# A two-layer hybrid decoder trunk: the order in which branch steps and projections are emitted, the lanes of the gated heads, and the width of the inverse steps

## The chip, the core and the metric

The kernel runs on one core of a Trainium2 chip. The metric is device time in microseconds (us) of one execution. Five engines work side by side, each in the order of its own instruction stream: TensorE (PE, with its weight loads shown as PEld), VectorE (DVE), ScalarE (ACT), GpSimd (POOL), and SyncE (SP), which issues nearly all DMAs.

## The reference

Sequence 512, width 1024, two layers, all in float32:

```python
for layer in range(DEPTH):
    u = rms_norm(h, norm_mix_g[layer])
    p_a, p_b, p_c, p_gate = _split(u @ w_in[layer], ...)
    y_a = rwkv7_branch(p_a, ...)    # 8 heads of 64, a linear recurrence over time
    y_b = hgrn2_branch(p_b, ...)    # 4 gated heads, keys and values of 128
    y_c = dsa_branch(p_c, cos, sin) # 8 heads of 64, top 128 keys chosen by an indexer
    branch = jnp.einsum('bsnc,ncd->bsnd', jnp.stack([y_a, y_b, y_c], axis=2), w_branch[layer])
    merged = jnp.sum(sigmoid(p_gate) * branch, axis=2)
    h = h + merged @ w_o[layer]
    h = h + conv_glu(rms_norm(h, norm_ffn_g[layer]), ...)  # up, 3-tap convolution, silu gate, down
return rms_norm(h, norm_final_g)
```

## The kernel before

All activations lie as 128 features by 512 time steps. A large product is made of three matmuls for each block of 128 input features (`big`, L293): a value is split into a high part and a residual (`split`, L264: ACT copies the high part, DVE or POOL subtracts), and high by high, high by residual and residual by high are summed in a bank of PSUM named `acc`. Such a matmul has 128x512 results; this text calls it a **wide matmul**. A projection of 128 columns is a block of 24 of them. Weights come in by SP as `wraw`; ACT makes `whi` and POOL `wlo` from them (`wload`, L270), five buffers of each, two pairs to a block.

A layer has a mixer and a feed-forward part. In the mixer two kinds of work are emitted into one stream by `interleave` (L62). **Fills** are made of wide matmuls: the projections of pair i of branch a (`pa0` to `pa3`), of branch c (`pc`) and of gated head i (`pb0` to `pb3`), the gates `gb` and `ga`, and the merges `mc`, `mb`, `ma`. **Lanes** are chains of small matmuls, each of which needs what DVE or ACT made of the one before: `pair_a` (L663, steps a0 to a3), `select` (s1 to s3), `attend` (c0 to c3) and `head_b` (L1004, b0 to b3). Lane steps write PSUM tiles named `lane`, all other wide work `acc`. Each `yield` of a lane gives a hand-written number, the us after which its next step may be emitted; PE's clock for that is a `Meter` that adds up a price for each matmul. While no lane is due, one fill goes on.

What emits first does not fix the order fully: the framework's scheduler then orders each engine's stream by priority, with work under `prio("feed")` ahead of the rest, and allots tile buffers (tag `t` has `NT` = 39 of them, 512 floats by 128 partitions each). At run time each engine takes its own stream strictly in order.

Names that the prediction uses:

- `pair_a`: `ars` (statistics by eleven DVE instructions of `rsqrt`, L248), `rx`, then `AR` and `BK` (L726 to L733), the masked 32x32 system `NU`/`TX`, its inverse by four doublings (L851 to L866: 32 small PE matmuls, a DVE multiply, 32 more, a DVE add and a 32x32-block transpose), a loop over eight chunks of 64 time steps (tiles `p1d`, `uf`, `VV`, `BKn`, `sbd`), and a normalization that ends in `yn` (L942), which PE transposes.
- `head_b`: nine levels of `bX` and `bE` (L1024 to L1086), four PE products of the upper levels, then `brs` and `bon` (L1115), again transposed by PE.
- Both layers begin with five projections made of the input before its norm is known (`feed["left"]`, L1240); meanwhile DVE makes the normed input `us`, then `uh` and `ul` from it. The feed-forward part does the same over four blocks (L1316), its `ul` on POOL from tiles `fu`.

## Time and profile before

| | us |
|---|---|
| median of three runs | 2244.77 |
| lowest and highest | 2241.41, 2249.47 |
| the profiled execution, its own time | 2235.76 |
| its span, first to last instruction | 2233.9 |
| PE busy in the span | 2113.2 |
| DVE, ACT, POOL busy | 1218.0, 1051.4, 944.3 |

The profiled execution is one run; its durations are set against its own 2235.76 us. A matmul's busy time reaches to the modelled end of its result, and the next one begins before that, so PE can be called busy and still lose time between starts. Two of the wide matmuls start 0.227 us apart when nothing is in their way.

### The profile page before, as it was taken

What the parts mean: (1) busy time and instruction counts of PE and PEld (TensorE: products, weight loads), DVE (VectorE), ACT (ScalarE), POOL (GpSimd) and SP (SyncE); (2) the same over time, 40 slices, a digit from 0 to 9 for tenths busy, and PEclk for the clock granted to TensorE, in tenths of its full rate; (3) what the DMA queues carried; (4) which work ended last, traced back from release to release, by engine and by line L of the source; (5) the groups of instructions that cost most, each with busy time, mean ns of one, the idle gap of its engine ahead of it and who ended that gap; (6) DMA issues with size and microseconds to landing.
All of it is one profiled execution on the core that took longest, in us unless ns stands there. A gap on an engine that the chain in (4) does not pass through costs nothing.

```text
span 2233.9 us, 41570 instructions
## 1 busy us (share of the span) xinstructions
PE 2113.2 (95%) x16598; PEld 1670.0 (75%) x16598; DVE 1218.0 (55%) x2744; ACT 1051.4 (47%) x2016; POOL 944.3 (42%) x739
## 2 busy tenths in 40 slices
PE   8998999998899999999999899999888999999997
PEld 6676777776687788888877677777666877888886
DVE  8668894467725633331185788753875356333211
ACT  6455555455433444443345564555563344444321
POOL 4231232232364666554442312222224547656563
PEclk9998999999999999999999999999999999999998
DMA  6221222222246233334332212222222552333332
GB/s 196 54 74 31 83 62 80 77 62 68 66 149 174 69 105 102 96 90 121 107 100 54 65 40 76 59 83 76 67 62 85 153 154 85 95 95 99 92 97 71
DMA packets 323506, 199.71 MB, mean 89 GB/s; under 512 B 10096, under 2 KB 304240, under 8 KB 323312
## 3 DMA queue, kind: packets, MB, share of 16 engines
q1 hardware_dynamic: 322592, 196.00, 30.3%
q8 instruction: 131, 2.15, 0.4%
q10 hardware_dynamic: 720, 1.05, 0.1%
q14 instruction: 63, 0.52, 0.1%
HBM read 178.14 MB, written 18.87 MB: 88 GB/s over the span
## 4 chain that ended last, share of the span: by engine, by line
PE 73%; DVE 17%; ACT 5%; issue 3%; POOL 2%; DMA 0%; SPq 0%; DVEq 0%; ACTq 0%; POOLq 0%
PE acc L55 59%; PE lane L55 12%; PE lane L59 1%; DVE bX L1048 1%; DVE sc L574 1%; DVE m L573 1%; DVE bX L1054 1%; DVE h L453 1%; ACT whi L265 1%; DVE bE L1052 1%; POOL ul L266 1%; DVE bF L1056 1%; POOL wlo L266 1%; DVE ars L254 0%; DVE rt L451 0%
## 5 line engine op out<-in xcount | busy, mean ns | idle before, releaser
L266 POOL TENSOR_TENSOR wlo<-wraw,whi 128x512 fp32r<-128x512 f32 (+1 forms) x602 | 789.6, 1313 | 1238.9 <-ACT whi L265 1129.9
L55 PE MATMUL acc<-uh,whi 128*128 128x512 f32 (+1 forms) x1776 | 727.7, 410 | 3.0 <-ACT uh L1263 2.9
L55 PE MATMUL acc<-ul,whi 128*128 128x512 f32 (+1 forms) x1776 | 712.3, 401 | 13.8 <-POOL ul L266 6.7
L55 PE MATMUL acc<-uh,wlo 128*128 128x512 f32 (+1 forms) x1776 | 708.1, 399 | 0.6 <-POOL wlo L266 0.6
L265 ACT CAST whi<-wraw 128x512 fp32r<-128x512 f32 (+1 forms) x604 | 368.9, 612 | 660.7 <-PE acc L55 558.9
L55 PEld LDWEIGHTS acc<-ul,whi 128*128 128x128 f32 (+1 forms) x1776 | 337.7, 190 | 80.7 <-POOL ul L266 8.9
L55 PEld LDWEIGHTS acc<-uh,whi 128*128 128x128 f32 (+1 forms) x1776 | 338.1, 190 | 79.2 <-issue 10.0
L55 PEld LDWEIGHTS acc<-uh,wlo 128*128 128x128 f32 (+1 forms) x1776 | 337.6, 190 | 69.9 <-POOL wlo L266 1.1
L1132 DVE SCALAR_TENSOR_TENSOR fc<-acc,vct,fc 128x511 f32<-128x511 f32 x80 | 60.0, 750 | 273.9 <-ACT fc L1131 273.9
L55 PE MATMUL acc<-hl,whi 128*128 128x512 f32 x416 | 162.0, 390 | 0.0
L55 PE MATMUL acc<-hh,wlo 128*128 128x512 f32 x416 | 162.0, 389 | 0.0
L55 PE MATMUL acc<-hh,whi 128*128 128x512 f32 x416 | 161.9, 389 | 0.0
L1151 DVE TENSOR_TENSOR h<-h,acc 128x512 f32<-128x512 f32 x16 | 11.0, 688 | 197.5 <-PE acc L55 197.5
L55 PEld LDWEIGHTS acc<-hl,whi 128*128 128x128 f32 x416 | 78.1, 188 | 16.3
L55 PEld LDWEIGHTS acc<-hh,wlo 128*128 128x128 f32 x416 | 78.1, 188 | 16.1
L55 PEld LDWEIGHTS acc<-hh,whi 128*128 128x128 f32 x416 | 78.1, 188 | 16.1
L55 PE MATMUL acc<-yl,whi 128*128 128x512 f32 x192 | 75.7, 394 | 3.3 <-POOL yl L266 3.2
L55 PE MATMUL acc<-yh,whi 128*128 128x512 f32 x192 | 76.2, 397 | 0.8 <-ACT yh L265 0.8
L55 PE MATMUL acc<-yh,wlo 128*128 128x512 f32 x192 | 75.3, 392 | 0.0
L55 PEld LDWEIGHTS lane<-bX 128*32 128x32 f32 (+2 forms) x1536 | 32.1, 116 | 42.2 <-issue 21.9
L55 PEld LDWEIGHTS lane<-TX,NU 32*32 32x32 f32 x4096 | 42.9, 107 | 25.8 <-issue 13.8
L1131 ACT ACTIVATE fc<-acc,vct 128x512 f32<-128x512 f32 x80 | 62.1, 776 | 0.0
(340 smaller groups left out, 3029.2 us busy)
## 6 DMA issues: line engine op xcount, KB each, us to landing
wraw<-in_w_in_dram SPq DMA_DIRECT2D x123, 512.0 KB, 3.8
wraw<-in_w_up_dram SPq DMA_DIRECT2D x88, 512.0 KB, 3.7
wraw<-in_w_down_dram SPq DMA_DIRECT2D x32, 512.0 KB, 3.9
wraw<-in_w_branch_dram SPq DMA_DIRECT2D x24, 512.0 KB, 3.4
gate<-rt SPq DMA_DIRECT2D x32, 256.0 KB, 2.0
rt<-gate SPq DMA_DIRECT2D x32, 256.0 KB, 2.9
wraw<-in_w_o_dram SPq DMA_DIRECT2D x16, 512.0 KB, 4.0
wraw<-in_w_down_dram SPq DMA_DIRECT2D x16, 384.0 KB, 3.4
```

What stands on the lines that cost most here:

```text
L55: return self.engine.matmul(out, lhsT, rhs, **kw)
L59: return self.engine.transpose(*args, **kw)
L265: act.copy(hi, src)
L266: eng.tensor_sub(lo, src, hi.bitcast(F32))
L453: dve.tensor_add(mg[d], mg[d], t_)
L573: dve.max(m8, sc[:, :S])
L574: dve.match_replace(sc[:, :S], m8, sc[:, :S], SENT)
L1048: dve.tensor_mul(Xu, qu, Eu)
L1052: dve.tensor_sub(El, end, Fl)
L1054: dve.tensor_mul(Xl, kl, El)
L1131: act.activation(c, ps, AF.Identity, bias=cw[:, 3, j:j + 1], scale=cw[:, 2, j:j + 1])
L1132: dve.scalar_tensor_tensor(c[:, 1:], ps[:, :T - 1], cw[:, 1, j:j + 1], c[:, 1:], op0=ALU.mult, op1=ALU.add)
```

## The change

`Timed` wraps DVE and ACT and adds up a price for each of their instructions (0.15 us plus 1.08 or 0.9 ns for each element of a partition). A lane's `yield` without a number now waits 0.35 us plus 1.1 times the vector work recorded since its last step; a few yields keep numbers, and the factor `PACE` of 0.9 is gone. A lane's first step comes 3.0 us after its inputs. Gates and merges yield 1.0 after each tile of 128 columns, and the next fill is then chosen anew, in the order of the list. Heads b0 and b2 now follow `select` in its lane, b1 and b3 follow `attend`; `pb0` waits for s3, `pa2` also for c2, `pb2` and `pb3` for the head two before. In `pair_a` each DVE step of the inverse takes all eight chunks in one instruction instead of four and four; `BK` is scaled in place after `Gs` on POOL, without tiles `BKs`; `bvh` and `bvl` are made later. The work beside late blocks (`side`) is issued under feed priority; a layer's start makes `us` after the first two late blocks instead of three, and the feed-forward part has six late blocks instead of four, with two tiles made beside each of the first four.

```diff
+class Timed:
+        def call(*args, **kw):
+            n = max(math.prod(a.shape[1:]) for a in (*args, *kw.values()) if isinstance(a, bass.AP))
+            self.t += self.base + self.per * n
+            return f(*args, **kw)
...
-def interleave(meter, lanes, fills):
+def interleave(meter, vectors, lanes, fills):
...
+        if wait is None:
+            wait = LATENCY + SHARE * (sum(v.t for v in vectors) - v0)
         return meter.t - t0, wait
...
-                lane[1], lane[2], lane[3] = make(), name, max(now, lane[3])
+                lane[1], lane[2], lane[3] = make(), name, max(now + START, lane[3])
...
-            lane[3] = now + (wait or 0.0) * PACE
+            lane[3] = now + max(wait, 0.0)
...
+            if wait:
                 fill = None
...
-BURST, PACE = 0.3, 0.9
+BURST, LATENCY, SHARE, START = 0.3, 0.35, 1.1, 3.0
...
+    dve, act = Timed(nc.vector, 0.15, 1.08e-3), Timed(nc.scalar, 0.15, 0.9e-3)
...
             nc.sync.dma_start(dst[d], t_)
+            yield 1.0
...
             r = use(ps)
-        if late:
-            feed["side"](feed["left"])
+            if late:
+                feed["side"](feed["left"])
...
-            for g in range(2):
-                dve.tensor_mul(X[:, 4 * g:4 * g + 4], quarter(px, g), bc(f"low{m}"))
-            yield 0.9
+            dve.tensor_mul(X, both(px), bc(f"low{m}"))
+            yield
...
-            for g in range(2):
-                cg = slice(4 * g, 4 * g + 4)
-                dve.tensor_add(Tt[:, cg], Tt[:, cg], quarter(pt, g))
-                dve.transpose(U[:, cg], Tt[:, cg])
-            yield 0.3
-            if next(parts, 0) is None:
-                yield 1.2
+            dve.tensor_add(Tt, Tt, both(pt))
+            dve.transpose(U, Tt)
+            next(parts, 0)
+            yield
...
-        yield 2.5
 
         rs = mp.tile([P, 24], F32, name=f"ars{lane}")
...
-            yield 1.5
+            yield
             if m == 16:
...
-                for k in {4: range(0, 3), 3: range(3, 6), 2: range(6, 8)}.get(left, ()):
+                for k in {4: range(0, 4), 3: range(4, 8)}.get(left, ()):
...
+            heads_b = [(f"b{i}", lambda i=i: head_b(lay, i, st, i % 2, l1, ys[1]), [f"pb{i}"]) for i in range(4)]
...
-                [(f"s{t}", lambda t=t: select(st, t, l1), ["pc"]) for t in (1, 2, 3)],
+                [(f"s{t}", lambda t=t: select(st, t, l1), ["pc"]) for t in (1, 2, 3)] + heads_b[0::2],
...
-                + [(f"b{i}", lambda i=i: head_b(lay, i, st, i % 2, l1, ys[1]), [f"pb{i}"]) for i in range(4)],
+                + heads_b[1::2],
...
-                for k in {3: range(0, 2), 2: range(2, 5), 1: range(5, 8)}.get(left, ()):
+                for k in {5: range(0, 2), 4: range(2, 4), 3: range(4, 6), 2: range(6, 8)}.get(left, ()):
...
-            feed.update(left=4, src=(gh, gl), rb=nrm.rb, tmp=lambda: fw.tile([P, T], F32, name="fc", bufs=6),
+            feed.update(left=6, src=(gh, gl), rb=nrm.rb, tmp=lambda: fw.tile([P, T], F32, name="fc", bufs=6),
```

Three places in the order show what that moves. The first is PE's stream late in a mixer, the upper levels of the last gated head, b3 of layer 0, before (`acc` rows are wide matmuls, `bX` rows the products of a level):

```order
L55 MATMUL lane_7057<-bX 64x64 x4
L55 MATMUL acc<-uh_519,whi 128x512
L55 MATMUL acc<-ul_527,whi 128x512
L55 MATMUL acc<-uh_519,wlo 128x512
L55 MATMUL lane_7077<-bX 128x128 x2
L55 MATMUL acc<-uh_520,whi 128x512
L55 MATMUL acc<-ul_528,whi 128x512
L55 MATMUL acc<-uh_520,wlo 128x512
L55 MATMUL acc<-uh_521,whi 128x512
L55 MATMUL acc<-ul_529,whi 128x512
L55 MATMUL acc<-uh_521,wlo 128x512
L55 MATMUL acc<-uh_522,whi 128x512
```

And PE's stream at the same levels of head b2 now, which runs beside the inverse of pair a3 (`TX,NU` rows):

```order
L55 MATMUL lane_6119<-bX 64x64 x4
L55 MATMUL lane_6180<-TX,NU 32x32 x32
L55 MATMUL lane_6215<-cst,av 128x128 x4
L55 MATMUL lane_6267<-TX,NU 32x32 x32
L55 MATMUL acc<-uh_519,wlo 128x512
L55 MATMUL acc<-uh_520,whi 128x512
L55 MATMUL acc<-ul_528,whi 128x512
L55 MATMUL lane_6319<-TX,NU 32x32 x21
L55 MATMUL lane_6233<-bX 128x128 x2
L55 MATMUL lane_6319<-TX,NU 32x32 x11
L59 MATMUL lane_6354<-cst,BK 128x128 x4
L55 MATMUL acc<-uh_520,wlo 128x512
```

Heads stood alone at the end of the mixer with wide matmuls between their levels; now one of them shares its stretch with the inverse of a pair. Counted in the whole order of layer 0, the three steps from a level of 32 to those of 64, 128 and 256 have 129 wide matmuls between them over the four heads before (11, 3, 14; 25, 0, 12; 12, 15, 12; 15, 3, 7), and 204 now (21, 15, 12; 50, 16, 18; 11, 3, 1; 18, 12, 27). Before `yn` stand 20 to 31 wide matmuls before (20, 31, 3 after other lane work, 30 with lane work among them) and 24, 19, 16 and 21 now; before `bon` 19 each before, and 15, 16, 11 and 21 now, some with lane work among them. The stream changes between `acc` and other matmuls 1045 times before and 949 times now. PE has 12185 instructions in both, DVE 2650 and 2518.

The second place is DVE's stream at the start of layer 0. Before (`late` takes a late block out of PSUM, `us` is the normed input, `ul` its residual that the next projection reads):

```order
L266 TENSOR_TENSOR gl<-gd,gh 128x512
L650 TENSOR_TENSOR ws<-wa,ws 64x512
L472 TENSOR_TENSOR late<-acc,nrb 128x512
L652 TENSOR_TENSOR as<-wa,as 64x512
L415 SCALAR_TENSOR_TENSOR us<-h_86,vct,nrb 128x512
L636 SCALAR_TENSOR_TENSOR ar<-late,vct,ar 128x511
L415 SCALAR_TENSOR_TENSOR us<-h_87,vct,nrb 128x512
L472 TENSOR_TENSOR late<-acc,nrb 128x512
L266 TENSOR_TENSOR ul_526<-us,uh_518 128x512
```

And now (L76 is the wrapper's call, so one line stands for all):

```order
L76 SCALAR_TENSOR_TENSOR us<-h_86,vct,nrb 128x512
L76 SCALAR_TENSOR_TENSOR us<-h_87,vct,nrb 128x512
L76 TENSOR_TENSOR wul<-wug,wuh 128x384
L76 TENSOR_SCALAR gd<-gd 128x512
L76 TENSOR_TENSOR gl<-gd,gh 128x512
L76 TENSOR_TENSOR ul_526<-us,uh_518 128x512
L76 TENSOR_TENSOR ws<-wa,ws 64x512
L76 TENSOR_TENSOR ul_527<-us,uh_519 128x512
```

The first `ul` came behind `gl` and seven more instructions; it now comes right behind `gl`, with the last two `us` moved ahead, and the `late` of the projections r, k and v behind all eight `ul`.

The third place is POOL's stream at the start of the feed-forward part of layer 0. Before:

```order
L266 TENSOR_TENSOR ul_8321<-fu,uh_8313 128x512
L266 TENSOR_TENSOR ul_8322<-fu,uh_8314 128x512
L266 TENSOR_TENSOR wlo<-wraw,whi 128x512
L266 TENSOR_TENSOR ul_8323<-fu,uh_8315 128x512
L266 TENSOR_TENSOR wlo<-wraw,whi 128x512
L266 TENSOR_TENSOR ul_8324<-fu,uh_8316 128x512
L266 TENSOR_TENSOR ul_8325<-fu,uh_8317 128x512
L266 TENSOR_TENSOR hl_8433<-fc,hh_8432 128x512
L266 TENSOR_TENSOR wlo<-wraw,whi 128x512
L266 TENSOR_TENSOR ul_8326<-fu,uh_8318 128x512
L266 TENSOR_TENSOR ul_8327<-fu,uh_8319 128x512
L266 TENSOR_TENSOR wlo<-wraw,whi 128x512 x3
```

And now:

```order
L291 TENSOR_TENSOR ul_8245<-fu,uh_8237 128x512
L291 TENSOR_TENSOR ul_8246<-fu,uh_8238 128x512
L291 TENSOR_TENSOR ul_8247<-fu,uh_8239 128x512
L291 TENSOR_TENSOR ul_8248<-fu,uh_8240 128x512
L291 TENSOR_TENSOR wlo<-wraw,whi 128x512
L291 TENSOR_TENSOR ul_8249<-fu,uh_8241 128x512
L291 TENSOR_TENSOR wlo<-wraw,whi 128x512
L291 TENSOR_TENSOR ul_8250<-fu,uh_8242 128x512
L291 TENSOR_TENSOR wlo<-wraw,whi 128x512
L291 TENSOR_TENSOR ul_8251<-fu,uh_8243 128x512
L291 TENSOR_TENSOR hl_8353<-fc,hh_8352 128x512
L291 TENSOR_TENSOR wlo<-wraw,whi 128x512 x3
```

The same operations stand there; the residuals `ul` moved ahead of weight residuals `wlo`, and the wide matmuls that read the last `ul` now come two blocks later.

## Rows read from the trace of the kernel before

**Rows 1.** The page's first part: busy time, share of the span, instructions.

```profile
PE 2113.2 (95%) x16598; PEld 1670.0 (75%) x16598; DVE 1218.0 (55%) x2744; ACT 1051.4 (47%) x2016; POOL 944.3 (42%) x739
```

**Rows 2.** Busy time by stretch: both mixers, then 100 us of feed-forward.

```profile
core 0: us, PE busy (x) PEld busy (x) DVE busy (x) ACT busy (x) POOL busy (x), PEclk, DMA share, GB/s
...
20.00:705.00 685.00, 637.79 (x6473) 492.03 (x6473) 461.89 (x1181) 340.34 (x713) 228.12 (x181) 0.97 0.29 84
...
1098.00:1810.00 712.00, 662.61 (x6588) 512.55 (x6586) 470.89 (x1177) 365.18 (x742) 236.70 (x189) 0.98 0.29 82
...
900.00:1000.00 100.00, 100.00 (x442) 82.78 (x442) 33.75 (x46) 45.65 (x74) 60.58 (x47) 1.00 0.32 94
```

**Rows 3.** PE's waits, whole span: total us, times, longest.

```profile
PE lane L55 <- DVE bX L1054: 20.3, 27, 1.9
PE lane L59 <- DVE yn L942: 15.4, 8, 2.8
PE lane L55 <- DVE BK L732: 12.8, 5, 3.8
PE lane L59 <- DVE bon L1115: 12.1, 8, 2.2
PE acc L55 <- POOL ul L266: 6.7, 2, 3.4
PE acc L55 <- DVE ul L266: 5.1, 2, 4.6
PE lane L55 <- DVE sbd L927: 4.0, 4, 1.3
...
PE lane L55 <- ACT asq L684: 2.4, 1, 2.4
```

**Rows 4.** PE in the 13 stretches of lowered clock: us, busy, clock; one, and all.

```profile
70.65:80.89 10.24, 10.24 (x96) 0.51 0.02 4
...
sum 88.74, PE 80.48; mean PE 6.19
```

**Rows 5.** PE's timeline, start and length: from lane matmuls back to wide ones.

```profile
386.50 0.38 PE L59 MATMUL lane<-cst,pr 128*128 128x128 f32 x2
386.64 0.48 PE L55 MATMUL acc<-uh,wlo 128*128 128x512 f32 x1
386.96 0.39 PE L55 MATMUL acc<-uh,whi 128*128 128x512 f32 x1
```

**Rows 6.** The timeline from a pair's last step to its `yn`.

```profile
373.33 0.65 ACT L938 ACTIVATE asq<-Y 128x512 f32<-128x512 f32 x1
...
376.71 1.29 POOL L266 TENSOR_TENSOR wlo<-wraw,whi 128x512 fp32r<-128x512 f32 x1 [3.63 <-ACT whi L265]
376.74 1.29 DVE L254 SCALAR_TENSOR_TENSOR ars<-ars 128x8 f32<-128x8 f32 x1
...
379.40 0.66 PE L59 MATMUL lane<-cst,yn 128*128 128x128 f32 x4 [1.42 <-DVE yn L942]
```

**Rows 7.** DVE's groups by line and shape: busy us, mean ns, idle before.

```profile
L1048 DVE TENSOR_TENSOR bX<-bq,bE 128x256 f32<-128x256 f32 x72 | 48.8, 678 | 18.5 <-ACT bE L1047 18.1
...
L862 DVE TENSOR_TENSOR TX<-TX,lane 128x128 f32<-128x128 f32 x64 | 15.7, 279 | 14.2 <-PE lane L55 14.1
...
L595 DVE CUSTOM_DVE_ANT_0 pr<-lane,sc 128x256 f32<-128x256 f32 x16 | 6.6, 420 | 0.2
```

**Rows 8.** The timeline where the late blocks of a feed-forward part end.

```profile
776.65 3.40 POOL L266 TENSOR_TENSOR ul<-fu,uh 128x512 fp32r<-128x512 f32 x2
780.01 4.65 POOL L266 TENSOR_TENSOR wlo<-wraw,whi 128x512 fp32r<-128x512 f32 x3
...
778.41 0.80 PE L55 MATMUL acc<-ul,whi 128*128 128x512 f32 x1 [3.35 <-POOL ul L266]
```

**Rows 9.** The timeline where the late blocks of layer 0 end.

```profile
45.64 0.68 DVE L266 TENSOR_TENSOR ul<-us,uh 128x512 fp32r<-128x512 f32 x1
...
46.37 0.79 PE L55 MATMUL acc<-ul,whi 128*128 128x512 f32 x1 [4.62 <-DVE ul L266]
```

**Rows 10.** PE's timeline at the first step that reads `BK`, pair a0.

```profile
70.23 0.73 PE L55 MATMUL lane<-AR,BK 64*32 64x32 f32 x63 [3.69 <-DVE BK L732]
```

More of the change, by code (lines that the diff above doesn't have):

```diff
@@ L59, in transpose, with __init__, __getattr__ @@
         return self.engine.transpose(*args, **kw)
-def interleave(meter, lanes, fills):
+class Timed:
+    def __init__(self, engine, base, per):
+        self.engine, self.base, self.per, self.t = engine, base, per, 0.0
+    def __getattr__(self, name):
+        f = getattr(self.engine, name)
+        if "dma" in name:
+            return f
+        def call(*args, **kw):
+            n = max(math.prod(a.shape[1:]) for a in (*args, *kw.values()) if isinstance(a, bass.AP))
+            self.t += self.base + self.per * n
+            return f(*args, **kw)
+        return call
+def interleave(meter, vectors, lanes, fills):
     done, now, run = set(), 0.0, 0.0
     lanes = [[list(l), None, None, 0.0] for l in lanes]
-    todo, fill = list(fills), None
+    todo, fill = [[*f, None] for f in fills], None
     def step(gen):
-        t0 = meter.t
+        t0, v0 = meter.t, sum(v.t for v in vectors)
         try:
@@ L75, in step @@
         except StopIteration:
-            wait = None
+            return meter.t - t0, -1.0
+        if wait is None:
+            wait = LATENCY + SHARE * (sum(v.t for v in vectors) - v0)
         return meter.t - t0, wait
@@ L82, in interleave @@
                 name, make, _ = lane[0].pop(0)
-                lane[1], lane[2], lane[3] = make(), name, max(now, lane[3])
+                lane[1], lane[2], lane[3] = make(), name, max(now + START, lane[3])
                 done.add("+" + name)
         if fill is None:
-            for i, (name, make, needs) in enumerate(todo):
-                if all(n in done for n in needs):
-                    fill = (name, make())
-                    todo.pop(i)
+            for entry in todo:
+                if all(n in done for n in entry[2]):
+                    entry[3] = entry[3] or entry[1]()
+                    fill = entry
                     break
@@ L97, in interleave @@
             run += cost
-            lane[3] = now + (wait or 0.0) * PACE
-            if wait is None:
+            lane[3] = now + max(wait, 0.0)
+            if wait < 0:
                 done.add(lane[2])
@@ L103, in interleave @@
         elif fill:
-            cost, wait = step(fill[1])
+            cost, wait = step(fill[3])
             now += cost
             run = 0.0
-            if wait is None:
+            if wait < 0:
                 done.add(fill[0])
+                todo.remove(fill)
+            if wait:
                 fill = None
@@ L474, in project @@
             r = use(ps)
-        if late:
-            feed["side"](feed["left"])
-            if feed["left"] == 0:
-                uh, ul = feed["then"]()
+            if late:
+                feed["side"](feed["left"])
+                if feed["left"] == 0:
+                    uh, ul = feed["then"]()
         return r
@@ L752, in bc, with both @@
         def bc(name):
-            return cc(name).unsqueeze(1).to_broadcast([P, 4, 32])
+            return cc(name).unsqueeze(1).to_broadcast([P, NCH, 32])
+        def both(ps):
+            return ps[:, :256].rearrange("p (c t) -> p c t", t=32)
         def quad(fn):
@@ L780, in pair_a @@
                           tile_position=(rows.start, o.start))
-        act.copy(N, bank[:, :256].rearrange("p (c t) -> p c t", t=32))
-        for g in range(2):
-            cg = slice(4 * g, 4 * g + 4)
-            dve.transpose(Tt[:, cg], N[:, cg])
-            dve.tensor_mul(Tt[:, cg], Tt[:, cg], bc("low1"))
-            dve.tensor_add(Tt[:, cg], Tt[:, cg], bc("eye32"))
-            dve.tensor_mul(U[:, cg], N[:, cg], bc("up1"))
-            dve.tensor_add(U[:, cg], U[:, cg], bc("eye32"))
+        act.copy(N, both(bank))
+        dve.transpose(Tt, N)
+        dve.tensor_mul(Tt, Tt, bc("low1"))
+        dve.tensor_add(Tt, Tt, bc("eye32"))
+        dve.tensor_mul(U, N, bc("up1"))
+        dve.tensor_add(U, U, bc("eye32"))
+        yield 0.2
         for hd in range(2):
@@ L791, in pair_a @@
             act.copy(L21[o], p21[o])
-        BKs = [s2("BKs").rearrange("p (c a t) -> p c a t", a=2, t=CH) for _ in range(2)]
-        for g in range(2):
-            cg = slice(4 * g, 4 * g + 4)
-            pool.tensor_mul(BKs[g].rearrange("p c a t -> p c (a t)"), BK[g].rearrange("p c a t -> p c (a t)"),
-                            gam[:, cg, CH:CH + 1].to_broadcast([P, 4, P]))
-        yield 0.2
         Gs = [[s2("Gs").rearrange("p (c d) -> p c d", c=4) for _ in range(2)] for _ in range(2)]
@@ L809, in pair_a @@
                 dve.tensor_mul(Gs[hd][g], pg[hd].rearrange("p (c d) -> p c d", c=4), gmask)
-            yield 1.6
+            cg = slice(4 * g, 4 * g + 4)
+            bk = BK[g].rearrange("p c a t -> p c (a t)")
+            pool.tensor_mul(bk, bk, gam[:, cg, CH:CH + 1].to_broadcast([P, 4, P]))
+            yield
         VV = [s2("VV").rearrange("p (c d) -> p c d", c=4) for _ in range(2)]
@@ L853, in pair_a @@
                                                    tile_position=(o.start, o.start)))
-            for g in range(2):
-                dve.tensor_mul(X[:, 4 * g:4 * g + 4], quarter(px, g), bc(f"low{m}"))
-            yield 0.9
+            dve.tensor_mul(X, both(px), bc(f"low{m}"))
+            yield
             pt = mbank()
```

42 lines of the change are left out of this document (20 added, 22 removed).

## Prediction

> **What bounds the kernel now.** The page's first part comes first: PE is busy 95% of the span and no other engine above 55% [rows 1]. So the end is set by PE's stream, and the question is what PE's 2113 us of busy time hide. The windows by stretch answer it: in 100 us of feed-forward PE starts 442 wide matmuls, 0.226 us each, at full clock and with nothing missing; the two mixers, 685 and 712 us, hold PE busy for only 637.79 and 662.61 us [rows 2], so 47 + 49 = 96 us of plain idleness stand there. Everything that the change touches, but for the start of the feed-forward part, is in these mixers. Three more views say how PE loses there. The list of its waits names a lane step of DVE nearly each time: `bX`, `yn`, `BK`, `bon`, `sbd` together 64.6 us, and three waits of late blocks and layer starts another 14.2 [rows 3]. After such waits the granted clock falls to its lower level, 1.2 GHz: 13 stretches, 88.74 us long with 80.48 us of busy PE [rows 4]; at half speed that is about 40 us lost, which the busy share hides. And each return from lane matmuls to wide ones costs something: 0.32 us to the next start instead of 0.226 [rows 5].
>
> Why the chains are late is seen before `yn`: from `asq` to PE's transpose it takes 6.07 us, and a DVE instruction on eight numbers a partition takes 1.29 us, over the very time of a POOL subtraction that began 0.03 us earlier [rows 6]. DVE and POOL hold one another up, so a sum of DVE prices is short of the real chain.
>
> A rule of the Trainium skill bears on this: "SBUF — State Buffer", section "SBUF: two separate sides", calls the port pair that DVE and GpSimd share an exclusive lock, held for a whole instruction, with the loser fully blocked. The row agrees (1.29 us beside 1.29). It speaks against a recorded price that knows no POOL; the rival "waits move" below is what follows from it, and by that rule alone the sum for `yn` and `bon` would be nought.
>
> **The change part by part.** Prices are those of the profiled execution, 2235.76 us, which is 9.0 below the median of 2244.77; the gain is worked out against the one and taken off the other.
>
> *Head levels.* PE waits 20.3 us for `bX`, 27 times, 0.75 us each [rows 3]. The three upper gaps of the eight heads had 129 wide matmuls a layer between them and have 204 now. The 75 more are 17 us a layer at 0.226 [rows 2], more than the wait of 10 us a layer, but they fall unevenly: 11, 3 and 1 at b2 against 11, 3 and 14 at the worst head before. A level's DVE work is a 0.678 us `bX` and its like [rows 7], so three wide matmuls don't cover it. I leave one head of four at its present mean of 2.5 us (20.3 over eight heads) and give half as much again to the others: 20.3 to about 8, **gain 12**; ends 0 and 20.
>
> *`yn` and `bon`.* 27.5 us in 16 waits [rows 3]. The chain of 6.07 us [rows 6] wants 27 wide matmuls. Ahead of `yn` stand 24, 19, 16 and 21, so it would be short by 0.6, 1.7, 2.4 and 1.3 us, 12 us in two layers against 15.4. `bon` has 63 in a layer where it had 76; 13 × 0.226 × 2 = 6 us worse if bare, though lane work now stands among them. I take **gain 4**; ends −3 and 15.
>
> *`BK`.* 12.8 us in five waits [rows 3], of which the first, of pair a0, is 3.69 us [rows 10]. From its statistics to the first reader of `BK` the order now has 69 wide matmuls for 51; 18 × 0.226 = 4.1 us is just over that wait. `BK` is also scaled in place on POOL, one tile less to wait for. I leave 3 us: **gain 10**; ends 3 and 12.8.
>
> *Chunk loop.* `sbd` costs 4.0 us in four waits of at most 1.3 us [rows 3]; about six wide matmuls, 1.36 us, now stand between steps that had two to five. **Gain 4**; ends 0 and 4.
>
> *Layer start.* PE waits 4.62 us for the first `ul` in layer 0 [rows 9], 5.1 in both layers, and 2.4 for `asq` [rows 3]. `ul` comes right behind `gl` now, seven DVE instructions of some 0.68 us earlier, so 4.62 should go; but `late` of r, k and v now stands behind all eight `ul`, and `asq` of the first pair waits for these. Eight `ul` of 0.68 us [rows 9] are 5.4 us in which nothing else on DVE moves. I let 3.5 of the 7.5 us stay: **gain 4**; ends −2 and 7.5.
>
> *Feed-forward start.* The late block's `ul` costs 3.35 us in layer 0 [rows 8], 6.7 in both [rows 3]. Two more late blocks take the reader of that `ul` 48 wide matmuls away. But POOL does the same work in the same time: it passes its `ul` at 780.05 and then the first of three weight residuals at 780.01 + 1.55 = 781.6 [rows 8]. The second half of the sixth late block, 18 wide matmuls behind the place where PE stood ready (778.41 − 3.35 = 775.06), wants that residual at 779.1. So PE waits 2.5 us there, for `wlo` instead of `ul`: **gain 2**; ends 0 and 6.7.
>
> *Inverse.* A multiply of four chunks takes 0.279 us and there are 64 [rows 7], so two for each doubling; one of eight chunks is twice as wide, between 0.420 us (128x256, L595) and 0.678 us (128x256, `bX`, which reads two SBUF tiles) [rows 7]. I take 0.42, as L595 also reads a bank of PSUM. DVE saves 0.14 us a step, but PE's first half gets its result 0.14 us later. Half of it on the path or none is not seen in the rows: before these steps DVE stood idle 14.2 us for PE [rows 7], so PE was last and not DVE. **0**; ends −9 (64 steps of 0.14) and +3.
>
> *Fewer returns to wide work.* PE's stream changes between `acc` and others 1045 times before and 949 now: 48 returns fewer, at 0.32 − 0.226 = 0.09 us [rows 5] and as much again, at most, for the way out. At 0.13, **gain 6**; ends 4 and 9.
>
> *Clock.* Of the 13 low stretches [rows 4] nearly all begin behind a wait of over a microsecond, such as the 3.69 before 70.23 [rows 10], which is followed by 10.24 us at 0.51 [rows 4]. With the waits above cut by 36 us out of 79, I expect about six to stay: 7/13 of 40 us, **gain 22**; ends 5 and 35.
>
> Sum: 12 + 4 + 10 + 4 + 4 + 2 + 0 + 6 + 22 = 64 us. 2235.76 − 64 = 2172 for an execution like the profiled one; median 2244.77 − 64 = about **2181 us**.
>
> **The rivals.**
> *All covers hold.* The waits of rows 3 that the change aims at go wholly (78.8 us, less 6 that POOL keeps) and 35 us of clock come back, with 9 for returns: 117 us, 2128. For it: PE is bound nowhere else [rows 1]. Against it: gaps of one and three wide matmuls are in the order.
>
> *Waits move to DVE's queue.* Heads now stand beside the inverse of a pair. DVE's work there (a head's levels, the pair's rescaling and inverse) and POOL's weight residuals block one another as in rows 6; DVE falls behind once for each of the two or three such clusters of a layer, by my estimate up to 11 us for the cluster with gaps of 11, 3 and 1, and PE then waits under `bX` and `yn` as before, with the clock low behind it. The feed-forward gain, `BK` and the returns stay: 20 to 40 us, 2205 to 2225. For it: rows 6. Against it: DVE is busy only 462 of 685 us [rows 2].
>
> *Merged steps are bare.* The skill's page "Perfetto Trace Analysis", section "Optimizing Scalar/DVE Operations", says that where Scalar or Vector cause bubbles on other engines, breaking up instructions may let work be done sooner; the change does the reverse. Worked out from rows 7: 64 × 0.14 = 9 us, 2190; if the wide form takes 0.678, 64 × 0.40 = 26 us, 2207. The 14.2 us for which DVE waited for PE speak against it.
>
> *Slower: tile buffers run out.* Two heads' tiles now live beside a pair's and those of `attend`, from one pool of 39. An ACT or DVE instruction that must wait for a free tile holds what is queued behind it on that engine: on ACT the high parts of the weights, and with them PE's wide matmuls. A wait of 3.3 us in each of the 16 branches (eight pairs, eight heads), with half as much again at low clock (40 lost beside 79 waited [rows 3, 4]), is 16 × 4.9 = 79 us: 2181 + 79 = 2260. It decides from 4.0 us a branch, clock included, where the 64 forecast are gone, and from 4.4 it is slower by more than can be told. For it: the order does not show buffers at all. Against it: heads already ran two at a time before.
>
> *It doesn't do what it says.* The planner may price covers that PE doesn't need, so that neither waits nor clock change: within 7 us of now. The order shows the changed covers, which speaks against it.
>
> **How the numbers follow.** About 0.3%, 7 us, is what a measurement of this kernel can tell from no change (the runs before lie between 2241.41 and 2249.47). Chances: forecast 0.48; all covers hold 0.14; waits move 0.17; merged steps bare 0.06; no effect 0.05; slower 0.10. Faster is 0.48 + 0.14 + 0.17 + 0.06 = 0.85. The range takes in the first four, 2120 to 2232 with the terms' ends: low by the covers' rival and some 8 us of other gains, high by the waits' rival with its lower gain cut by another 7. What it leaves out is no effect and slower, 0.15.
>
> **What would show it.** Right: under PE's waits `BK` and `sbd` nearly gone, `bX` below 10 us, `yn` and `bon` still the largest; the feed-forward wait named `wlo` and near 2.5 us; six or seven low stretches, some 40 to 45 us; `acc` starts at 0.226 us unchanged. Wrong: mixers shorter by less than 20 us each; a new name on top of the waits (ACT `whi`, or a tile's release); DVE busy longer in the mixers than 462 and 471 us [rows 2]; low stretches as long as now with half the waits gone, which would say that the clock doesn't follow the waits.

## The result, and the profile after

The changed kernel takes 2218.45 us (median of 4 runs, 2214.93 to 2222.85) against 2244.64 before: a ratio of 0.9883, 95% interval 0.9855 to 0.9910. It is 26 us faster where 64 were forecast. The direction and the range held; the size is under half, and it lies where the rival "waits move" had put it (2205 to 2225).

The profiled executions differ by 15.1 us of span (2233.9 and 2218.8): the one before was 9 us faster than its median, the one after 2 us slower. What the traces below show is those 15 us; the other 11 are seen in the medians alone. First the page's busy times, and the windows of the two mixers and of the two feed-forward parts:

```profile
PE 2095.0 (94%) x16598; PEld 1666.8 (75%) x16598; DVE 1205.6 (54%) x2612; ACT 1044.4 (47%) x2016; POOL 948.8 (43%) x739
```

```profile
core 0: us, PE busy (x) PEld busy (x) DVE busy (x) ACT busy (x) POOL busy (x), PEclk, DMA share, GB/s
20.00:696.00 676.00, 626.14 (x6475) 487.89 (x6474) 452.52 (x1116) 338.24 (x713) 228.50 (x183) 0.99 0.29 85
1082.00:1799.00 717.00, 663.79 (x6590) 518.09 (x6589) 462.07 (x1109) 362.15 (x742) 238.14 (x190) 0.97 0.28 82
```

```profile
734.00:1098.00 364.00, 361.96 (x1602) 298.83 (x1601) 123.98 (x160) 152.84 (x249) 216.98 (x165) 1.00 0.35 101
1837.00:2081.00 244.00, 241.98 (x1072) 199.37 (x1071) 107.00 (x137) 114.71 (x185) 159.15 (x117) 1.00 0.32 95
```

The same pieces of work lasted 685 and 712 us in the mixers before [rows 2]. So one mixer is 9 us shorter and the other 5 us longer, and PE's idle time in both together rose, from 47.2 + 49.4 to 49.9 + 53.2 us. The feed-forward parts (the second without its down product, which took 119.7 us in both) lasted 369 and 249 us before and 364 and 244 now; from matmul to matmul they are 4.5 and 4.1 us shorter. The gain that was forecast for the mixers has stayed away; the one forecast at 2 us is the steadier half of what came.

PE's waits after, which answer to [rows 3] (total, times, longest; all of DVE and ACT now has the wrapper's line L76):

```profile
PE lane L59 <- DVE yn L76: 14.5, 8, 2.2
PE lane L55 <- DVE sbd L76: 14.2, 16, 3.0
PE lane L55 <- DVE bX L76: 12.8, 12, 1.9
PE lane L55 <- DVE TX L76: 8.7, 14, 1.0
PE acc L55 <- POOL yl L291: 7.1, 8, 1.6
PE lane L59 <- DVE bon L76: 6.2, 7, 1.5
PE lane L59 <- ACT pr L76: 5.3, 8, 1.2
PE lane L55 <- ACT asq L76: 4.9, 2, 2.6
PE lane L55 <- DVE Gs L76: 4.8, 4, 1.6
PE lane L55 <- ACT VV L76: 4.3, 10, 0.8
PE acc L55 <- POOL wlo L291: 4.3, 5, 1.6
PE acc L55 <- DVE ul L76: 3.4, 9, 0.6
...
PE lane L55 <- DVE BK L76: 1.8, 3, 0.8
```

`BK` is 11.0 us less than before, `bX` 7.5, `bon` 5.9. `sbd` is 10.2 more, and `TX`, `pr`, `yl` and `Gs`, which stood too low in the list of before to be quoted, are near the top. The waits have changed their names, and their sum has not fallen: the whole list comes to 109.5 us in 109 waits before and to 112.9 us in 132 now. The long ones did become fewer: 14 of over 2 us, 41.7 us together, before; 10, 23.4 us together, now.

The clock, in all stretches at the lower level ahead of the last norm (length, busy PE, clock), which answers to [rows 4]:

```profile
core 0: us, PE busy (x), PEclk, DMA share, GB/s
...
56.93:63.76 6.83, 6.83 (x21) 0.52 0.21 45
...
1442.74:1463.22 20.48, 20.26 (x200) 0.51 0.10 26
...
sum 61.45, PE 60.35; mean PE 5.49
```

There are 11 stretches, not six; one in layer 1 is a third of the whole. They hold 20.1 us less of busy PE than before, at half speed some 10 us, reckoned as the 40 us of the prediction were. PE is busy for 18.2 us less in the whole span and idle for 3.1 us more; so 8 us of the shorter busy time are not the clock. The 48 fewer returns to wide matmuls would be 4 to 9 us of that at the forecast's prices; no run shows them by themselves.

One trace is one draw of the clock, as the last section shows. All executions give a steadier figure: the mean granted clock is 0.976 in the 64 of the kernel before that the sets below hold, and 0.9835 in the four of the changed one. The difference over 2220 us is some 16 us; by this estimate the clock is the larger part of the 26.

### The profile page after: what moved, and what is told of

Read it like the earlier page. It is cut to its first block, busy times and chain, and to the rows that moved or that the text cites. A ratio compares the mean times of both kernels' runs of the same rounds, so it can differ in the third digit from the quotient of the medians.

```text
span 2218.8 us, 41407 instructions
## 1 busy us (share of the span) xinstructions
PE 2095.0 (94%) x16598; PEld 1666.8 (75%) x16598; DVE 1205.6 (54%) x2612; ACT 1044.4 (47%) x2016; POOL 948.8 (43%) x739
## 3 DMA queue, kind: packets, MB, share of 16 engines
q10 hardware_dynamic: 720, 1.05, 0.1%
## 4 chain that ended last, share of the span: by engine, by line
PE 66%; DVE 20%; ACT 6%; issue 4%; POOL 2%; DMA 1%; SPq 0%; DVEq 0%; ACTq 0%; POOLq 0%
PE acc L55 53%; PE lane L55 11%; DVE sc L76 2%; DVE ars L76 2%; DVE h L76 2%; DVE bX L76 2%; PE lane L59 1%; DVE m L76 1%; DVE brs L76 1%; POOL wlo L291 1%; DVE rt L76 1%; DMA yr<-y 1%; ACT whi L76 1%; DVE ul L76 1%; POOL ul L291 1%
## 5 line engine op out<-in xcount | busy, mean ns | idle before, releaser
L55 PE MATMUL acc<-uh,whi 128*128 128x512 f32 (+1 forms) x1744 | 715.3, 410 | 2.7 <-ACT uh L76 2.7
L55 PE MATMUL acc<-ul,whi 128*128 128x512 f32 (+1 forms) x1744 | 691.0, 396 | 3.4 <-DVE ul L76 3.4
L55 PE MATMUL acc<-uh,wlo 128*128 128x512 f32 (+1 forms) x1744 | 690.0, 396 | 0.6 <-POOL wlo L291 0.6
L76 ACT CAST whi<-wraw 128x512 fp32r<-128x512 f32 (+1 forms) x604 | 368.5, 611 | 603.6 <-PE acc L55 504.2
L76 DVE SCALAR_TENSOR_TENSOR fc<-acc,vct,fc 128x511 f32<-128x511 f32 (+1 forms) x152 | 113.9, 749 | 255.8 <-ACT fc L76 253.1
L55 PE MATMUL acc<-hh,wlo 128*128 128x512 f32 x448 | 174.9, 390 | 3.7 <-POOL wlo L291 3.7
L55 PE MATMUL acc<-hl,whi 128*128 128x512 f32 x448 | 174.5, 390 | 0.0
L55 PE MATMUL acc<-hh,whi 128*128 128x512 f32 x448 | 174.4, 389 | 0.0
L76 DVE TENSOR_TENSOR h<-h,acc 128x512 f32<-128x512 f32 x32 | 22.0, 688 | 234.7 <-PE acc L55 234.7
L76 ACT ACTIVATE pr<-pr,cst 128x128 f32<-128x128 f32 (+3 forms) x128 | 69.9, 558 | 41.9 <-DVE cst L76 41.7
L291 POOL TENSOR_TENSOR hl<-fc,hh 128x512 fp32r<-128x512 f32 x44 | 58.5, 1329 | 11.9 <-ACT hh L76 11.7
```

The costliest lines, as they stand in the source:

```text
L55: return self.engine.matmul(out, lhsT, rhs, **kw)
L76: return f(*args, **kw)
L291: eng.tensor_sub(lo, src, hi.bitcast(F32))
```

## The experiments

Every run is set against the kernel before, run beside it on the same chip (2240 to 2243 us in these sets; 2244.64 beside the changed kernel's 2218.45). A ratio is that to the kernel before of the same set. Where times of two sets are compared as they stand, a difference of under some 5 us says nothing. Three questions were asked: what the late blocks carry, whether the wide inverse or the order costs what is missing, and which edit of the planner carries the rest.

### The late blocks

`late_alone` is the kernel before with the feed-forward lines shown here and with the changed layer start (`us` after two late blocks, `side` under feed priority); `ffn_four` is the changed kernel without the feed-forward lines:

```diff
-                for k in {3: range(0, 2), 2: range(2, 5), 1: range(5, 8)}.get(left, ()):
+                for k in {5: range(0, 2), 4: range(2, 4), 3: range(4, 6), 2: range(6, 8)}.get(left, ()):
-            feed.update(left=4, src=(gh, gl), ...
+            feed.update(left=6, src=(gh, gl), ...
```

> The kernel before with only the edits to the late blocks: six instead of four at the feed-forward start with two tiles made beside each of the first four, the normed input two blocks earlier at a layer's start, and that side work under feed priority; lanes, planner and inverse as before. Theory: the feed-forward parts carry almost half of the measured 26 us. There the two traces differ by 415.9 - 409.1 and 413.7 - 408.9, 11.6 us; so 2244.6 - 12 = about 2232 us (2228 to 2236), the wait for ul gone, about 1.6 us for wlo in each part, no stretch of low clock in either feed-forward part. Rival: the part is worth the 2 us of the prediction's term (and up to 4 at the layer's start), the rest came from the planner: 2238 to 2243 us.

> The changed kernel with the feed-forward part's start as before: four late blocks, tiles made beside three of them. Theory: six late blocks are worth about 9 us wherever the mixers stand (in the two traces, from the start of the feed-forward part to its end, 4.5 us a layer): the wait for ul comes back with 6 to 7 us, wlo falls below 1 us, low clock returns behind it, and the time is 2218 + 9 = 2227 (2223 to 2232). Rival: the part is worth the 2 us of the prediction's term: 2218 to 2222.

`late_alone` took 2234.25 us against 2240.11, ratio 0.9973 (0.9958 to 0.9989): 6 us. `ffn_four` took 2225.15 us, 6.7 above the changed kernel (10 by the ratios, 0.9927 and 0.9883). So the late blocks are worth 6 to 10 us, at least three times the term of 2. In the traces their feed-forward parts are 8.6 us shorter in `late_alone` than before, and only 2.8 us longer in `ffn_four` than in the changed kernel. The wait itself went as the prediction worked it out, from `ul` to `wlo`, a little shorter than the 2.5 us forecast (changed kernel, layer 0; 1.63 in layer 1 too):

```profile
769.87 0.50 PE L55 MATMUL acc<-hh,wlo 128*128 128x512 f32 x1 [1.63 <-POOL wlo L291]
```

Much of the rest is clock: no stretch at the lower level lies in the feed-forward parts now (their clock reads 1.00 in the windows above), where there was one of 6.8 us in each before. The layer start gave nothing in `late_alone`: `ul` fell there from 5.1 to 2.0 us, and `asq`, whose inputs come behind it, rose from 2.4 to 5.6.

### The wide inverse, or the order

`inverse_halves` undoes the merged steps, the multiply shown here and the add and transpose likewise:

```diff
-            dve.tensor_mul(X, both(px), bc(f"low{m}"))
+            for g in range(2):
+                dve.tensor_mul(X[:, 4 * g:4 * g + 4], quarter(px, g), bc4(f"low{m}"))
```

> The changed kernel with the multiply, add and transpose of each doubling again made for four and four chunks; all else changed. The recorded vector work of such a step grows by 0.3 us, so the emission order changes with it. Theory: PE's waits for TX, 8.7 us now and 1.4 before, come from the wide instruction, which gives the first half later; then they fall below 3 us and the time by about 5 us, to 2213. Rival: they come from too few wide matmuls between the steps while other vector work stands ahead in the queue; then they stay between 5 and 11 us and the time within 5 us of 2218.

2194.72 us, ratio 0.9798 (0.9771 to 0.9824): 24 us faster than the changed kernel, five times what the theory asked, while `TX` fell little. An instruction in two parts is also recorded at a higher price, which moves PE's stream. Two runs part the two. One keeps the wide instructions and adds their halves' price to the record (`dve.t += 0.15` for each of the three operations); the other has halves at the wide price. In PE's streams the two kernels of a column below differ in some 40 to 50 of 8000 rows, those of a row in 2500 to 2700 (runs of equal matmuls counted as one).

> The changed kernel, whose wide inverse steps are recorded at the price of the two halves (0.15 us more for each of the three operations), so that PE's stream is that of the kernel with halves (2195 us) but for some 70 rows, while the instructions stay wide. Theory: what the halves gained lies in the emission order; then this is near 2195, within 6 us. Rival: it lies in the instructions, since PE goes on after the first half; then it is near 2218.

> The reverse: halves as instructions, recorded at the price of one wide step, so that PE's stream is that of the changed kernel but for some 80 rows. Theory (order): near 2218, within 6 us. Rival (instructions): near 2195.

| | order of the wide price | order of the halves' price |
|---|---|---|
| wide instructions | 2218.45 | 2196.10 |
| halves | 2221.16 | 2194.72 |

The order is worth 22 to 26 us (18 to 27 by the ratios), the instructions at most 3 (8 by the ratios, with intervals that overlap). So no gain or loss can be told from the width of the inverse steps; the sum had put it at nothing, and a wide step does take the 0.42 us that it went by. The rule that the prediction cited against it (the Trainium skill, "Perfetto Trace Analysis", "Optimizing Scalar/DVE Operations") does not bite here: the wide form loses 1.4 us in the one order and gains 2.7 in the other.

### How much is the chance of one order

If 0.15 us on a recorded price moves 25 us, the factor on it must do the same. Only the number changes (`SHARE`, 1.1 in the changed kernel):

> The changed kernel with a factor of 1.05 on the recorded vector work in place of 1.1, a step's wait being some 0.1 us shorter. Theory: which steps come to lie beside which fills is so sensitive that neighbours scatter; then the time differs from 2218 by 8 us or more, to either side, with PE's waits at other names. Rival: the time follows the length of the waits smoothly; then it is within 5 us of 2218, with the same names on top of PE's waits.

> The changed kernel with the factor at 1.15. The same two theories: scatter, 8 us or more from 2218 to either side, not in line with the run at 1.05; or smooth, within 5 us, and the three factors in one line.

> The changed kernel with a factor of 1.0 on the recorded vector work. Scatter: anywhere from 2185 to 2225, not foretold by 2191 at 1.05. Smooth: the waits grow with the shorter distance and the time is a little above 2191, 2192 to 2200.

> The changed kernel with a factor of 0.9. Scatter: 2185 to 2235. Smooth: a lane's step is now due before its own recorded work is over, PE's waits add up to 15 us more than at 1.05 (94 us), and the time is 2200 to 2210.

> The changed kernel with a factor of 0.8. So far 1.15, 1.1, 1.05, 1.0 and 0.9 gave 2200, 2218, 2191, 2198 and 2184. Scatter: between 2180 and 2220, without a line. Smooth with a trend down: 2175 to 2184. If a step due before its own work is over costs: PE's waits above 115 us and the time above 2200.

> The changed kernel with a factor of 0.95, between 0.9 (2184) and 1.0 (2198). Scatter: anywhere from 2180 to 2220. Smooth between its neighbours: 2184 to 2198.

| factor | 1.15 | 1.10 | 1.05 | 1.00 | 0.95 | 0.90 | 0.80 |
|---|---|---|---|---|---|---|---|
| us | 2200.1 | 2218.5 | 2191.3 | 2197.9 | 2207.1 | 2183.8 | 2217.7 |

No line runs through them. 0.95 was to lie between its neighbours and lies above both. The mean of the seven is 2202 us, they spread over 35 us, and the changed kernel is, with 0.80, the slowest of them. The fastest, at 0.90, beats both kernels: 2183.79 us, ratio 0.9744 (0.9721 to 0.9767). Its waits and its lowered clock:

```profile
PE lane L55 <- DVE bX L76: 19.0, 19, 2.2
PE lane L59 <- DVE yn L76: 14.6, 8, 4.2
PE lane L55 <- DVE p1d L76: 9.2, 10, 1.4
PE lane L55 <- DVE sbd L76: 7.8, 10, 1.1
...
PE lane L55 <- DVE TX L76: 3.4, 6, 1.6
```

```profile
core 0: us, PE busy (x), PEclk, DMA share, GB/s
...
sum 23.87, PE 22.86; mean PE 3.81
```

It waits under other names again (`bX` as long as before, `p1d` new), but it is at the lower clock for 24 us in six stretches, where the changed kernel is for 61 in eleven. How long PE waits in all and how often the clock falls are two things: it has waits of up to 4.2 us, 99.7 us in all, where the kernel at 1.05 waits for only 92.7 and is at the lower clock for 58.

### Where one new wait comes from

Half of the largest new wait, `sbd` (eight of its 16 waits, 7.1 of 14.2 us), stands in the chunk loop of a layer's first pair. DVE, ACT, POOL and PE there, in the changed kernel:

```profile
129.48 0.69 DVE L76 TENSOR_TENSOR rt<-rt,sin 128x512 f32<-128x512 f32 x1 [1.26 <-ACT rt L76]
130.21 1.80 DVE L76 TENSOR_TENSOR qf<-ra,rt 128x512 f32<-128x512 f32 x1
131.93 0.45 DVE L76 COPY sbd<-lane 64x64 f32<-64x64 f32 x2
```

```profile
126.94 2.50 ACT L76 COPY rt<-rt 32x512 f32<-32x512 f32 x4
129.47 0.62 ACT L76 CAST whi<-wraw 128x512 fp32r<-128x512 f32 x1
130.00 0.26 ACT L76 COPY VV<-lane 64x128 f32<-64x128 f32 x1
```

```profile
130.17 1.29 POOL L291 TENSOR_TENSOR wlo<-wraw,whi 128x512 fp32r<-128x512 f32 x1 [2.49 <-ACT whi L76]
```

```profile
130.30 0.49 PE L55 MATMUL lane<-VV,BKn 128*128 128x128 f32 x2 [0.35 <-ACT VV L76]
...
132.52 0.35 PE L55 MATMUL lane<-sbd,AR 128*128 128x128 f32 x1 [1.03 <-DVE sbd L76]
```

The lane's own work here is 0.26 us on ACT and 0.45 on DVE. Ahead of it in the two queues stands the rotation of a branch c projection (`rt`, `qf`), which the fill brought and no lane's record counts; and `qf`, whose like takes 0.69 us, takes 1.80 beside a POOL instruction of 1.29. That is once more what [rows 6] showed. The Trainium skill says of the shared ports ("SBUF — State Buffer", "SBUF: two separate sides") that the one that comes second waits for the whole of the first; here `qf` ended 0.55 us after the POOL instruction. The loop's three numbers were doubled for the first pair alone:

```diff
-            yield 0.85
+            yield 1.7 if pr == 0 else 0.85
```

> The changed kernel with the three numbers of the chunk loop doubled for the first pair of each layer alone (0.85, 0.85, 0.95 to 1.7, 1.7, 1.9). In the first pair's loop PE waits eight times about 0.9 us for sbd and eight times 0.35 to 0.8 for VV, where the rotation of the branch c projections stands ahead on ACT and DVE. Theory: a lane's wait must hold what the fills put into the vector queues, not its own work alone; then these waits go with the longer distance, sbd from 14.2 to below 6 us and VV from 4.3 to below 2, and the sum of PE's waits falls by about 10 us, time 2208. Rival: wide matmuls are a fixed sum, and what this loop gets is missing later; then sbd and VV fall just as much, but the sum of PE's waits stays within 5 us of 115 and the time within 5 us of 2218.

`sbd` fell from 14.2 to 3.3 us and `VV` from 4.3 to 1.4, so the longer distance does take these waits away. The time rose to 2229.59 us (ratio 0.9948, 0.9931 to 0.9966). These went up instead (its list of waits):

```profile
PE lane L55 <- DVE bX L76: 17.1, 17, 2.8
PE lane L59 <- DVE bon L76: 14.4, 8, 3.3
PE acc L55 <- ACT yh L76: 8.8, 7, 2.0
```

The rival holds but for its time: wide matmuls are a fixed sum, the waits come to 114.2 us in all for 112.9, and what one loop gets is missing later, here at the last heads. The 11 us that it cost lie within the scatter of the orders; a cause of their own is not shown.

Another new wait, `yl`, was put down to the last head's output coming back too late, and the last two merges exchanged:

```diff
-                ("mb", ..., ["b3", "gb", "mc"]),
-                ("ma", ..., halve), ["a3", "ga", "mb"]),
+                ("ma", ..., ["a3", "ga", "mc"]),
+                ("mb", ..., halve), ["b3", "gb", "ma"]),
```

> The changed kernel with the last two merges of a layer exchanged: ma (branch a) before mb (the gated heads). Up to there the order is the same. In the changed kernel the last head ends with 42 wide matmuls left before mb, which reads that head's output back from memory. Theory: the waits for yl, 7.1 us (3.2 before), come from this, since y is stored, read back and split on POOL in the meantime; with ma first they fall to 0 to 3 us and the time by 4 to 10 us, to 2208 to 2214. Rival: yl is late because POOL is busy with weight residuals at any merge; then it stays at 5 to 8 us and the time within 4 us of 2218.

That theory fell: `yl` stayed at 7.4 us and the time at 2223.74 (ratio 0.9915, 0.9881 to 0.9949). Whether POOL's weight residuals or the late end of both branches does it stays open; at the factors 0.80 to 1.05 the traces have no wait for `yl`, at 1.15 they have 6.7 us and the time is 2200.

### Which edit carries the mixers

Heads back in one lane, at two factors (the projections `pb` again wait only for the head before; these lines are left out here):

```diff
-                [(f"s{t}", ...) for t in (1, 2, 3)] + heads_b[0::2],
+                [(f"s{t}", ...) for t in (1, 2, 3)],
-                + heads_b[1::2],
+                + heads_b,
```

> The changed kernel with all four gated heads again one after another in the lane of attend, and their projections waiting as before; planner, late blocks and inverse stay changed. Theory: heads in two lanes are what cut bX and bon from 32 to 19 us; undone, these return to 28 to 34 us, the waits for TX and Gs fall by some 5, and the time is 5 to 12 us above 2218. Rival: a head beside an inverse costs as much as it saves (TX, Gs and yl rose by 16 us); then bX and bon rise and TX, Gs and yl fall by the same, and the time stays within 5 us of 2218 or falls.

> The kernel with the factor of 1.05 (2191 us), its four gated heads again one after another in one lane. Theory: the two lanes are worth what they were at 1.1, where undoing them cost 22 us, because wide matmuls that lie unused between merges and gates go between head levels; then this takes 2191 + 22 = 2213 (2207 to 2220). Rival: the 22 us were a matter of the one order too; then it lies within 8 us of 2191 or beyond 2223.

2240.77 and 2236.13 us: 22 and 45 us above the same kernels with two lanes, and no longer faster than the kernel before by more than the late blocks carry (ratios 1.0000 and 0.9976). Yet `bX`, which the first theory saw rise to 28 us or more with `bon`, stayed at 12.8; what rose was `bon`, `yh` and `uh`, at the mixer's end. Then the other way, two lanes in the kernel before, whose fills go on to their end once begun:

> The kernel before, with its hand-written waits, halves and four late blocks, and only the heads in two lanes with what their projections wait for. Theory: two lanes carry most of the gain whatever sets the waits, since undoing them cost 22 us at a factor of 1.1 and 45 at 1.05; then this gains 15 to 40 us on the kernel before, 2200 to 2225. Rival: they pay only together with the recorded waits and the choice of fills at tile boundaries, without which levels of two chains come due at once with nothing between them; then it is within 8 us of 2240 or slower.

2259.57 us, ratio 1.0077 (1.0056 to 1.0098): slower. So two lanes pay only with something else. The nearest candidates are the recorded waits and the fills left at tile boundaries; the last pair takes only the latter away:

```diff
                 todo.remove(fill)
-            if wait:
                 fill = None
```

> The changed kernel (factor 1.1) in which a fill, once begun, goes on to its end as before, so that gates and merges are not left at a tile's boundary for another fill. Theory: leaving them is what lets two lanes of heads pay, since the projections of the next head come in between gates; without it the time is 12 us or more above 2218, 2230 or more, as in the kernel with hand-written waits and two lanes (2260). Rival: the recorded waits do it; then it lies between 2190 and 2225, as other factors do.

> The same at the factor 0.9 (2184 us with the boundaries). Theory: 2205 us or more. Rival: between 2180 and 2200.

2266.70 and 2273.44 us, 48 and 90 us above the kernels with boundaries, ratios 1.0098 (1.0073 to 1.0123) and 1.0134. This is the largest effect of all. At the factor 1.10, its PE at the end of layer 0's last head, and the wide matmuls in the stretch (windows with `acc` alone: length, PE busy and count):

```profile
646.94 2.24 PE L55 MATMUL lane<-bX 128*64 128x64 f32 x12 [3.16 <-DVE bX L76]
650.75 2.08 PE L55 MATMUL lane<-bX 128*128 128x256 f32 x4 [1.57 <-DVE bX L76]
...
655.72 0.39 PE L55 MATMUL lane<-bvi,pbd 128*128 128x128 f32 x2
661.63 1.12 PE L59 MATMUL lane<-cst,bon 128*128 128x128 f32 x4 [5.53 <-DVE bon L76]
```

```profile
639.00:662.00 23.00, 0.00 (x0) 0.00 (x0) 0.00 (x0) 0.00 (x0) 0.62 0.07 23
```

In the changed kernel the last 23 us up to its last `bon` read:

```profile
605.00:628.00 23.00, 14.51 (x54) 10.20 (x54) 1.37 (x2) 0.60 (x1) 0.93 0.17 58
```

No wide matmul is left, and the last heads run bare, at a clock of 0.62. The fill that is missing is the merge of branch c (`mc`, eight tiles), whose result no head or pair needs. Its last instruction (`h<-h,acc`) and the last one of b3's projection (`bg<-bg,acc`), without boundaries:

```profile
553.77 0.69 DVE L76 SCALAR_TENSOR_TENSOR h<-h,acc 128x512 f32<-128x512 f32 x1 [5.97 <-PE acc L55]
617.94 0.69 DVE L76 SCALAR_TENSOR_TENSOR bg<-bg,acc 128x512 f32<-128x512 f32 x1 [2.19 <-ACT bg L76]
```

And in the changed kernel:

```profile
567.70 0.69 DVE L76 SCALAR_TENSOR_TENSOR bg<-bg,acc 128x512 f32<-128x512 f32 x1
633.23 0.69 DVE L76 SCALAR_TENSOR_TENSOR h<-h,acc 128x512 f32<-128x512 f32 x1 [4.14 <-PE acc L55]
```

Without boundaries `mc` was emitted in one go, its tiles ending between 446 and 554 us, while the projections of b2 and b3, which heads wait for, stood behind it until 618. Left after each tile, it gave three tiles up to 517 us, then b3's projection went ahead, and five tiles remained for the last heads. The gates are not that stock: 15 of their 16 tiles are done by 300 us in the changed kernel, all by 309 us without boundaries. In `one_lane_105` the last `bon` comes at 640 us, after a bare wait of 4.9 us, with `mc` used up at 627 and the last gate's tile at 635; there it is the heads that end too late. `hand_two_lanes` is not explained by this: its last head still has 51 wide matmuls in its last 23 us, and why it is slower stays open.

## Why the prediction was right in sign and wrong in size

By its own steps:

- **What bounds the kernel** holds: PE at 94%, full rate in the feed-forward parts, the loss in the mixers.
- **The step that failed** is the sum of the waits. They were to fall by 36 us, each by its own covers; in all they rose, from 109.5 to 112.9 us, and the mixers, each of which was to be over 20 us shorter, are 9 shorter and 5 longer. **New waits elsewhere** were no term at all: `TX`, `yl`, `pr` and `Gs` make 25.9 us after, for 6.4 before. The sum took each wait away by itself, as if covers came from nowhere. They come from one stock, which the runs without boundaries and the doubled loop show running out at the end.
- **`BK`** 11.0 for 10 and the **inverse** at nothing came as worked out; so did **`wlo` in place of `ul`** (1.6 us for 2.5 in each part), whose parts gained more by the clock. **Returns** can be 4 to 9 for 6, not shown by themselves. **Head levels** gave 7.5 for 12; the worst head before was b3 (15, 3, 7), not the one with 11, 3 and 14, and nothing hangs on that.
- **`yn` and `bon`** gave 6.8 for 4, but by luck: `yn`, which was to gain some 3, gained 0.9, and `bon`, feared to be up to 6 worse, gained 5.9.
- **Chunk loop** is a term with the wrong sign: forecast −4, measured +10.2. Its step counted wide matmuls between steps (about six for two to five) and took the lane's own work as what they must cover. What fills had put into DVE's and ACT's queues was left out, though the part on `yn` had said that a sum of DVE prices falls short. The first pair's loop shows it.
- **Layer start** was forecast at 4 and gave 0.6: of 7.5 us, `ul` at the starts keeps 2.0 and `asq` takes 4.9. That `asq` waits for what comes behind all eight `ul` had been seen, but was priced too low.
- **The clock** was forecast as 22 us from six stretches left. The two traces give some 10, with eleven, the granted clock of all executions some 16. It came without the fall in the waits that was to bring it; that fewer long waits did is argued, not shown. At 0.90 six stretches are left, and the time is 2184: the estimate of what can be had was near, not that of which order would have it.
- **An edit was not priced**: fills left at tile boundaries. The prediction went through levels, loops and starts where the order shows them, and had no line for this one, without which the two lanes lose more than the whole gain. Boundaries with one lane, and two lanes without boundaries, gain nothing clear beyond the late blocks.
- **The rivals.** The time is that of "waits move to DVE's queue", and vector queues are part of it, but not at the place named: the largest new wait is beside branch c's projections, not beside a head and an inverse, and DVE is busy for 9 us less in each mixer than before. "Slower" was given a shortage of tiles; what makes the plan without boundaries slower is a stock of fills that runs out.
- **The point forecast** of 2181 is 3 us under the best of seven factors and 21 under their mean. Of the 37 us between forecast and result, so much (21) was too much hope in the covers, and 16 is the order that this one factor gave, if their mean is taken as what the plan is worth. The prediction had no width for that at all; its range held the time by way of the rival.

Not settled: why neighbouring orders differ by up to 35 us, place by place. The runs show that it is the order, not the instructions, and that the names of the waits change with it; no one wait is the whole difference. The lowered clock changes with the order and also from one execution to the next.

## What to carry to other kernels

Price a planner's change as a draw from a family of orders: move its constants by a few per cent and time the neighbours, before reading a cause into one order or judging another edit by it. Work that nothing waits for is the stock that covers the last chain; count how much of it is left when that chain ends, and check what an edit does to that count before counting covers one by one. A lane's distance that holds only its own work leaves a wait behind what others have queued on the vector engines; but a longer one for a single loop took its covers from other places here, and gained nothing.

## What the runs showed of the hardware

That a POOL instruction stretches a DVE one was known from the trace before; new is how far it goes on a full tile (0.69 to 1.80 us beside 1.29), and how regularly. Take the DVE instructions of the changed kernel's trace that combine two 128x512 inputs outside PSUM: 114 of them began with no POOL instruction under way, and took 0.65 to 0.70 us even where one began beside them. Of the 72 that began during one, 71 ended 0.54 to 0.56 us after it.

The same instructions, in two layers, met the clock differently: in the changed kernel layer 1 spent 20.48 us at the lower level behind `AR,BK` products of its third pair, after waits of 1.17 and 0.74 us, where layer 0, with 1.19 and 0.85 us in the same place, stayed at full clock. So did two executions of one order. The first 2973 matmuls of PE's stream are the same in the changed kernel and in `ffn_four`, and the waits among them are 26.4 and 27.2 us; they took 359.0 us with two stretches at the lower level, and 365.5 us with seven. At 188 us both wait for `yn` equally long; the changed kernel (first rows) goes on at full clock, `ffn_four` (second rows) falls to the lower level (0.53 from 188.25 to 191.66):

```profile
188.46 0.63 PE L59 MATMUL lane<-cst,yn 128*128 128x128 f32 x4 [2.06 <-DVE yn L76]
...
189.62 0.40 PE L55 MATMUL acc<-uh,whi 128*128 128x512 f32 x1
```

```profile
187.64 0.63 PE L59 MATMUL lane<-cst,yn 128*128 128x128 f32 x4 [2.06 <-DVE yn L76]
...
189.06 0.63 PE L55 MATMUL acc<-uh,whi 128*128 128x512 f32 x1
```

What decides that the rows do not show. A count of such stretches from one trace is one draw; the mean clock of several executions is the safer figure.
